# Two late experts' rows, the final norm's factors and a POOL drain in the tail of a mixture-of-experts layer

## The chip, the core and the metric

The kernel runs on one core of a Trainium2 chip. The metric is device time of one execution in microseconds (us). Work is spread over five engines: PE (matrix products), DVE and ACT (elementwise work), POOL (here mostly gathers and scatters) and SP (which only issues transfers). The 16 DMA engines of the core move data. Each engine works through its own list of instructions in order; semaphores make it wait for others.

## What is computed

One layer of a diffusion backbone over 512 latent tokens with 1024 features: a gated linear attention mixer, then a grouped top-2 mixture of 16 experts, then a final RMSNorm. Only the last two concern this change:

```python
for e in range(N_EXPERTS):
    he = jax.nn.silu(h @ w1[e]) * (h @ w3[e])
    out = out + gates[:, e:e + 1] * (he @ w2[e])
...
x = x + g2 * f.reshape(bsz, t, D_MODEL)
...
return _rmsnorm(x, final_g)
```

`_rmsnorm` divides each row by the root of its mean square and multiplies it by `final_g`. A token goes to two experts, so a row of `x` gets two sums, and its norm needs both.

## The kernel before, in words

Experts are sorted by how many tokens they got; the first run with many rows, the last two (the late ones, here **p** and **q**, list places 14 and 15) hold at most 32 rows each. For each expert POOL gathers its rows, PE multiplies them by gate and up weights ("up", halves a and b) and by the down weights ("down"), DVE scales the result by gate and `g2`, and POOL adds it by an indirect scatter to the accumulator `accd` in DRAM (L1106). SP streams the weights, 1 MB a load (L688). `load_unit` gives each load a dependency on the landing of the load three before it, so at most three are in flight. The scheduler also uses eight completion lanes (DMAHW0 to DMAHW7) in turn for transfers issued by SP and ACT: a transfer that takes a lane waits until the lane's last one has landed.

For p and q the scatter is left out. The tail, whose order on all engines is written out by hand, does this instead:

- `finish_consts` (on ACT and its queue) lays out `g2` and loads `final_g` to all 128 partitions with one transfer (L1330) into a buffer that the compiler calls `srg`.
- `late_consts` builds 0/1 matrices: `hot` (which accumulator row belongs to which late row) and `same` (which row of p is the same token as which row of q). A key is transposed on PE and compared on DVE.
- `finish_load` reads `accd` back in four tiles of 128 rows (L1341, B and su) once the scatter of expert 13, the last one that goes to `accd`, has landed. `squares` (ACT, L1344), `finish_scale` and `finish_out` (DVE, L1351; store on SP, L1352) norm these 512 rows and store them. The rows of p and q are stored there too, still without the late sums.
- `late_rows` picks the accumulator rows of p and q out of the four tiles by products with `hot`. `late_other` adds, by a product with `same`, the other late expert's sum where both have the token.
- `late_out` norms the rows of p and q and stores them over the earlier ones with two indirect stores from POOL (L1401). They write to `out`, so the first waits for the landing of the four tile stores, and the second for the landing of the first. The norm is over quarters of a row that lie in four partition groups, and a product with `SELP` sums their squares.

A `G.drain()` (L1435) stands in the tail's code. It depends on nothing, and in the built program of before it sits near the start of POOL's list. After the tail comes a loop that runs zero times for these inputs (L1513) and the end of the program (L1556), where POOL has a drain of its own.

Of the kernel before, what the change touches and what calls it, by code (L numbers as in the profile page):

```python
# [10 lines left out]
BF16 = mybir.dt.bfloat16  # L11
I32 = mybir.dt.int32
U8 = mybir.dt.uint8
AF = mybir.ActivationFunctionType
OP = mybir.AluOpType
# [3 lines left out]
P = 128  # L19
D = 1024  # L20
# [12 lines left out]
def dit_kernel(ctx: ExitStack, tc: tile.TileContext, I, out):  # L33
# [12 lines left out]
    def bank(p=None):  # L46
        p = p or pa
        return p.tile([P, 512], F32, tag="bk", name="bk")
# [1266 lines left out]
    def index_for(g):  # L1315
        c0 = cols[order[g[0]]][0][0]
        c1 = cols[order[g[-1]]][-1][0] + 1
        index_of(c0, tiles[c0:c1], lambda e: zp[:, :, e - NS], vals, wide=g[0] == 2)

    ss3, rstd3 = R("ss3", [4]), R("rstd3", [4])  # L1320
    fin = {}

    def finish_consts():
        f, e = free.pop(0), free.pop(0)
        fin["g"], fin["j"] = f[:, 0:1024], f[:, 1024:2048]
        fin["y"] = [u[:, h * 1024:h * 1024 + 1024] for u in (free.pop(0), free.pop(0)) for h in range(2)]
        fin["h"], fin["g2"], *fin["late"] = [e[:, k * 256:k * 256 + 256] for k in range(6)]
        fin["hot"] = [e[:, 1536 + 128 * k:1664 + 128 * k].rearrange("p (t s) -> p t s", t=4) for k in range(2)]
        fin["same"] = [e[:, 1792 + 128 * k:1920 + 128 * k] for k in range(2)]
        nc.scalar.dma_start(fin["g"], I["final_g"].rearrange("(o n) -> o n", o=1).partition_broadcast(P))  # L1330
        lay("g2", g2b)

    def lay(name, src):
        A = P // tiles[-1][2]
        for a in range(A):
            q, n = slice(P // A * a, P // A * (a + 1)), D // A
            S.copy(fin[name][q, 0:n], src[q, a * n:a * n + n])

    def finish_load(ts=range(4)):
        for t in ts:  # L1340
# [23 lines left out]
    for a in range(QA):  # L1364
        ia = ident[:, a * P // QA:(a + 1) * P // QA].unsqueeze(1).to_broadcast([P, QA, P // QA])
        V.tensor_add(sv, sv, ia) if a else V.tensor_copy(sv, ia)
    lrs, lsq, key = R("lrs", [2]), m1[:, 2:4], m1[:, 0:2]

    def late_consts(ts):
        c = NTL - 2  # L1370
        V.tensor_copy(key, gix2[:, c:c + 2])
        for k in range(2):
            for t in range(4):
                V.tensor_scalar(fin["hot"][k][:, t], iot[:, 0:32], zp[:, t, ND - 2 + k:ND - 1 + k], None, op0=OP.is_equal)
            pt = bank(pb)[:, 0:P]
            PE.transpose(pt, key[:, k:k + 1].to_broadcast([P, P]), ident)
            V.tensor_scalar(fin["same"][k], pt, key[:, 1 - k:2 - k], None, op0=OP.is_equal)

    def late_rows(ts, k):
        for i, t in enumerate(ts):  # L1380
# [1 line left out]
                t.rows, t.z = bank()[:, 0:t.n], fin["late"][2 + i]  # L1382
            t.groups(t.rows, fin["hot"][i][:, k], lambda a: fin["y"][k][:, a * t.n:a * t.n + t.n], k == 0, k == 3)

    def late_other(ts, i):
        pt = bank()[:, 0:ts[i].n]
        PE.matmul(pt, fin["same"][i], ts[1 - i].y, start=True, stop=True)
        return pt

    def late_out(ts):  # L1390
        for i, t in enumerate(ts):
            S.activation(mo.tile([P, 512], BF16, tag="ohx", name="jk3", bufs=NO)[:, 0:t.n], t.z, AF.Square, accum_out=lsq[:, i:i + 1])
        pt = bank(pb)
        PE.matmul(pt[:, 0:2], SELP, lsq, start=True, stop=True)
        rsqrt(lrs, pt[:, 0:2], 2, 1.0 / D, "x")
        for i, t in enumerate(ts):
            V.scalar_tensor_tensor(t.z, t.z, lrs[:, i:i + 1], fin["h"][:, 0:t.n], op0=OP.mult, op1=OP.mult)
            late_store(t)

    def late_store(t):  # L1400
        G.indirect_dma_start(out=parts(out[0], t.A), out_offset=bass.IndirectOffsetOnAxis(ap=t.idx, axis=0), in_=t.z, in_offset=None,  # L1401
# [2 lines left out]
    with tc.manual_schedule(engines={G.engine}):  # L1404
        ex = [Expert(cols[order[0]], True)]
        weights()
        ex.append(Expert(cols[order[1]]))
        ranked()
        for i in range(NE - 1):
            if i == 1:  # L1410
                ex[0].down(wts[0])
                with tc.issue_after(ex[0].tls[0].last.ins):
                    rest()
                    index_for(range(2, 4))
                ex[0].store()
            ex[i].up(wts[i], "a")
            while i and len(ex) < min(NE, i + 3):
                ex.append(Expert(cols[order[len(ex)]]))
            if i > 1:
                ex[i - 1].down(wts[i - 1])  # L1420
            ex[i].up(wts[i], "b")
            if i % 2 and i + 3 < NE:
                index_for(range(i + 3, min(i + 5, NE)))
            if i:
                ex[i - 1].scatter()

    finish_consts()
    tail = {G.engine, V.engine, S.engine, PE.engine, nc.sync.engine}
    with tc.manual_schedule(engines=tail):
# [2 lines left out]
        p.late, q.late = fin["late"][0:2]  # L1432
        q.by_exp = True
        pq = (p, q)
        G.drain()  # L1435
        late_consts(pq)
        p_.down(wts[NE - 2])
        S.preload_act_table_set("natural_log_exp_and_others")
        q_.up(wts[NE - 1], "a")
        load_unit(wts[NE - 1], regs[NE - 1], 4)  # L1440
        finish_load()
        for h in range(2):
            load_unit(wts[NE - 1], regs[NE - 1], 5, range(h, h + 1))
        S.copy(fin["late"][3], late_other(pq, 1))
        q_.up(wts[NE - 1], "b")
        q_.turn()
        for k in range(2):
# [6 lines left out]
            squares(k)  # L1454
            late_rows(pq, k)
        finish_scale(2)
        lay("h", fin["g"])
        V.tensor_add(p.z, p.y, p.rows)
        V.tensor_add(q.z, q.z, q.rows)
        finish_out(2)  # L1460
        q_.down(wts[NE - 1])
        V.tensor_add(q.z, q.z, q.y)
        V.tensor_add(p.z, p.z, late_other(pq, 0))
        finish_out(3)
        late_out(pq)


    ctx2 = ExitStack()
# [91 lines left out]
```

## Time and profile before

| | us |
|---|---|
| median of 3 runs (lowest to highest) | 661.37 (660.69 to 661.97) |
| the profiled execution | 660.54 |
| its span, first to last instruction | 658.7 |
| PE busy | 603.8 (92%) |
| DVE busy | 463.1 (70%) |
| ACT busy | 302.1 (46%) |
| POOL busy | 89.8 (14%) |

The profiled execution has 1.84 us around its span and is 0.83 us under the median. Rows of a timeline give start, duration, engine, line of the kernel, operation, what is written and read, count, and in brackets the idle time of the engine before and what ended it. A name with q behind it (SPq, POOLq) is the engine's sequencer.

### The profile page before, as it was taken

The numbers are of one execution on the slowest core, as the hardware profiler recorded it, in microseconds if no ns is written. First come the engines' busy times: TensorE is split into PE (matmuls) and PEld (weight loads), VectorE is DVE, ScalarE is ACT, GpSimd is POOL, SyncE is SP. The second block draws the span as 40 slices with busy tenths as digits, with TensorE's granted clock in tenths as the row PEclk, the third lists the DMA queues.
The fourth block names the chain that finished last, engine by engine and source line by source line (L and its number), as shares of the span: only waits on it lengthen the run. The fifth ranks groups of instructions, "written<-read, shape, count | busy, mean of one in ns | idle before, by whom it ended". The sixth has DMA issues, their size and how long they took to land. (4 is left out here: it accounts for less than half of the span.)

```text
span 658.7 us, 11293 instructions
## 1 busy us (share of the span) xinstructions
PE 603.8 (92%) x4266; PEld 415.1 (63%) x4266; DVE 463.1 (70%) x951; ACT 302.1 (46%) x512; POOL 89.8 (14%) x99
## 2 busy tenths in 40 slices
PE   3999999999999999999979989999999999999760
PEld 3777677776878878778757465446455657664320
DVE  5766599749976962664489398477799979994251
ACT  6334398266252334632441354345353657772150
POOL 3030000010100010013100232020321222331001
PEclk9999999999999999999979999999999999999985
DMA  8996572120235771577662989899999999999981
GB/s 275 341 350 208 194 253 65 66 65 3 90 106 194 256 254 49 208 256 291 256 237 63 402 306 360 336 343 344 369 378 400 368 345 365 401 387 365 325 336 44
DMA packets 50248, 168.87 MB, mean 256 GB/s; under 512 B 6738, under 2 KB 17100, under 8 KB 37136
## 3 DMA queue, kind: packets, MB, share of 16 engines
q1 hardware_dynamic: 43216, 156.26, 63.9%
q0 software_dynamic: 4880, 8.64, 5.5%
q10 hardware_dynamic: 2096, 3.23, 1.5%
q8 instruction: 34, 0.56, 0.3%
q14 instruction: 22, 0.18, 0.1%
HBM read 159.03 MB, written 12.30 MB: 260 GB/s over the span
## 5 line engine op out<-in xcount | busy, mean ns | idle before, releaser
L51 PE MATMUL bk<-wh,fh 128*128 128x512 f32 (+3 forms) x276 | 111.1, 409 | 0.7 <-ACT fh L56 0.4
L52 PE MATMUL bk<-wl,fh 128*128 128x512 f32 (+3 forms) x276 | 111.0, 404 | 0.0
L53 PE MATMUL bk<-wh,fl 128*128 128x512 f32 (+3 forms) x276 | 109.2, 400 | 0.5 <-DVE fl L57 0.5
L282 DVE TENSOR_TENSOR wl<-st,wh 128x512 fp32r<-128x512 f32 x60 | 39.8, 684 | 39.1 <-ACT wh L281 37.8
L56 ACT CAST wh<-su 128x1024 fp32r<-128x1024 f32 x45 | 46.7, 1047 | 39.7 <-PE bk L53 37.8
L281 ACT CAST wh<-st 128x512 fp32r<-128x512 f32 x60 | 35.9, 621 | 61.6 <-PE bk L53 51.1
L51 PEld LDWEIGHTS bk<-wh,fh 128*128 128x128 f32 (+3 forms) x276 | 50.1, 183 | 20.0 <-ACT wh L56 3.4
L52 PEld LDWEIGHTS bk<-wl,fh 128*128 128x128 f32 (+3 forms) x276 | 50.7, 184 | 16.0 <-DVE wl L57 2.5
L57 DVE TENSOR_TENSOR wl<-su,wh 128x1024 fp32r<-128x1024 f32 x45 | 54.5, 1221 | 8.1 <-ACT wh L56 6.7
L53 PEld LDWEIGHTS bk<-wh,fl 128*128 128x128 f32 (+3 forms) x276 | 50.5, 183 | 13.7 <-issue 1.2
L1106 POOL DMA_INDIRECT accd<-y,gix x15 | 34.3, 2290 | 157.9 <-DVE y L1166 86.8
L56 ACT CAST fx<-su 128x1024 fp32r<-128x1024 f32 x21 | 22.0, 1049 | 21.9 <-PE bk L53 21.7
L1202 PE MATMUL bk<-su,xg 128*32 128x256 f32 (+1 forms) x216 | 30.4, 457 | 1.5 <-DVE xg L1196 1.5
L57 DVE TENSOR_TENSOR fx<-su,fx 128x1024 fp32r<-128x1024 f32 x21 | 25.6, 1221 | 5.6 <-ACT fx L56 5.3
L51 PE MATMUL bk<-fx,fh 128*128 128x512 f32 (+3 forms) x68 | 27.9, 410 | 1.2 <-ACT fh L56 1.2
L52 PE MATMUL bk<-fx,fh 128*128 128x512 f32 (+3 forms) x68 | 27.4, 402 | 1.0 <-DVE fx L57 1.0
L53 PE MATMUL bk<-fx,fl 128*128 128x512 f32 (+3 forms) x68 | 26.6, 394 | 0.2 <-DVE fl L57 0.2
L1102 POOL DMA_INDIRECT xg<-h2d,gix x16 | 19.7, 1232 | 40.0 <-DVE pis L1005 15.4
L1202 PE MATMUL bk<-su,he 128*64 128x512 f32 (+1 forms) x136 | 21.6, 497 | 0.9 <-DVE he L1226 0.8
L250 POOL DMA_DIRECT2D mrd<-mrow x8 | 3.8, 487 | 129.4 <-DVE mrow L248 129.4
L52 PE MATMUL bk<-fl,wh 128*128 128x512 f32 x48 | 19.8, 412 | 0.0
L53 PE MATMUL bk<-fh,wl 128*128 128x512 f32 x48 | 19.7, 411 | 0.0
(486 smaller groups left out, 1284.9 us busy)
## 6 DMA issues: line engine op xcount, KB each, us to landing
su<-in_w_up_e_dram SPq DMA_DIRECT2D x23, 1024.0 KB, 8.3
su<-in_w_down_e_dram SPq DMA_DIRECT2D x21, 1024.0 KB, 7.9
su<-in_w_gate_e_dram SPq DMA_DIRECT2D x19, 1024.0 KB, 7.6
st<-in_gla_w_in_dram SPq DMA_DIRECT2D x10, 1024.0 KB, 5.4
QQ<-in_w_mod_dram SPq DMA_DIRECT2D x5, 1024.0 KB, 10.2
st<-in_w_gate_e_dram SPq DMA_DIRECT2D x5, 1024.0 KB, 8.1
st<-in_w_up_e_dram SPq DMA_DIRECT2D x5, 1024.0 KB, 9.4
B<-in_w_mod_dram SPq DMA_DIRECT2D x4, 1024.0 KB, 4.8
```

Source lines behind the costliest of these rows:

```text
L51: PE.matmul(o, ah, bh, start=first, stop=False)
L52: PE.matmul(o, ah, bl, start=False, stop=False)
L53: return PE.matmul(o, al, bh, start=False, stop=last)
L56: S.copy(hi, full)
L57: return V.tensor_sub(lo, full, hi.bitcast(F32))
L250: G.dma_start(mrd[4 * h_ + c4:4 * h_ + c4 + 1, :], mrow[32 * c4:32 * c4 + 1, :])
L281: S.copy(w[0][:, k], st[:, k])
L282: mark[0] = V.tensor_sub(w[1][:, k], st[:, k], w[0][:, k].bitcast(F32))
L1102: G.indirect_dma_start(out=xg, out_offset=None, in_=src, in_offset=bass.IndirectOffsetOnAxis(ap=idx, axis=0), bounds_check=n - 1, oob_is_e ...
L1106: G.indirect_dma_start(out=dst, out_offset=bass.IndirectOffsetOnAxis(ap=idx, axis=0), in_=y, in_offset=None, bounds_check=n - 1, oob_is_er ...
L1202: PE.matmul(o[s.w * a:s.w * a + s.w], l, r(a), start=first, stop=last, tile_position=(0, s.w * a))
```

## The change

Six edits, all in the tail:

1. `final_g` is loaded into one partition (4 KB in place of 512 KB), after `g2` is laid out. A new function, `finish_g`, spreads it to 128 partitions by two products with a row of ones and two copies from PSUM. It stands between p's down and q's up.
2. Only one `same` matrix is built (one transpose and one compare fewer). p's rows are stored with the accumulator's rows and p's own sum alone; q's rows get both sums. A token that both have is stored twice, the second time, by q's store, in full.
3. `late_out` is called for p and for q apart. p's call stands ahead of q's down.
4. The last `finish_out` stands straight behind the third, ahead of everything of q.
5. `lay("h", ...)`, which spreads `final_g` for the late rows, stands behind `finish_out`; on ACT it keeps its place.
6. `G.drain()` stands at the end of the block that orders POOL's list, behind expert 13's scatter.

```diff
+    one = raw2[0:1, :]
...
-        fin["g"], fin["j"] = f[:, 0:1024], f[:, 1024:2048]
+        fin["g"], fin["j"], fin["row"] = f[:, 0:1024], f[:, 1024:2048], f[0:1, 1024:2048]
...
-        nc.scalar.dma_start(fin["g"], I["final_g"].rearrange("(o n) -> o n", o=1).partition_broadcast(P))
+        nc.scalar.dma_start(fin["row"], I["final_g"].rearrange("(o n) -> o n", o=1))
+        V.memset(one, 1.0)
...
+    def finish_g():
+        for a in range(2):
+            sl = slice(a * 512, a * 512 + 512)
+            pt = bank()
+            PE.matmul(pt, one, fin["row"][:, sl], start=True, stop=True)
+            S.copy(fin["g"][:, sl], pt)
...
-            pt = bank(pb)[:, 0:P]
-            PE.transpose(pt, key[:, k:k + 1].to_broadcast([P, P]), ident)
-            V.tensor_scalar(fin["same"][k], pt, key[:, 1 - k:2 - k], None, op0=OP.is_equal)
+        pt = bank(pb)[:, 0:P]
+        PE.transpose(pt, key[:, 1:2].to_broadcast([P, P]), ident)
+        V.tensor_scalar(fin["same"][0], pt, key[:, 0:1], None, op0=OP.is_equal)
...
+    def late_out(t, i):
+        ss, n = m1[:, 2 + i:3 + i], t.n
+        S.activation(mo.tile([P, 512], BF16, tag="ohx", name="jk3", bufs=NO)[:, 0:n], t.z, AF.Square, accum_out=ss)
         pt = bank(pb)
+        PE.matmul(pt[:, 0:1], SELP, ss, start=True, stop=True)
+        rsqrt(lrs[i], pt[:, 0:1], 1, 1.0 / D, "x")
+        V.scalar_tensor_tensor(t.z, t.z, lrs[i], fin["h"][:, 0:n], op0=OP.mult, op1=OP.mult)
+        late_store(t)
...
+        G.drain()
...
-        G.drain()
         late_consts(pq)
         p_.down(wts[NE - 2])
         S.preload_act_table_set("natural_log_exp_and_others")
+        finish_g()
         q_.up(wts[NE - 1], "a")
...
-        lay("h", fin["g"])
         V.tensor_add(p.z, p.y, p.rows)
         V.tensor_add(q.z, q.z, q.rows)
         finish_out(2)
+        finish_out(3)
+        lay("h", fin["g"])
+        late_out(p, 0)
         q_.down(wts[NE - 1])
         V.tensor_add(q.z, q.z, q.y)
-        V.tensor_add(p.z, p.z, late_other(pq, 0))
-        finish_out(3)
-        late_out(pq)
+        late_out(q, 1)
```

The first place is SP's list, at the weights of q: `su_2693` is the up weights of q's half a, the two `st` are half b, `su_2696` is half of its down weights. Names in brackets are the semaphores waited for, and the transfer of `final_g` sits on lane DMAHW1 before and on DMAHW2 now. One piece of the difference:

```order
 L688 DMA su_2700<-in_w_gate_e_dram 128x2048 [waits DMAHW5_49,PE_49]
 L688 ISA
-L688 DMA su_2693<-in_w_up_e_dram 128x2048 [waits DMAHW6_49,DMAHW1_49,PE_49]
-L688 ISA
-L688 DMA st<-in_w_gate_e_dram 128x2048 [waits DMAHW7_49,DVE_49]
+L688 DMA su_2693<-in_w_up_e_dram 128x2048 [waits DMAHW6_49,PE_49]
+L688 ISA
+L688 DMA st<-in_w_gate_e_dram 128x2048 [waits DMAHW7_49,DMAHW2_49,DVE_49]
```

The wait for `final_g` has moved from the load of half a's up weights to the next load.

The second place is DVE's list at the end of the tail: L1351 (L1360 in the change) is `finish_out`, L1234 q's sum, L1462 and L1463 the additions to the late rows, L136 to L129 the roots, L1397 (L1400) the scaling of the late rows. Before:

```order
L1351 SCALAR_TENSOR_TENSOR su_2692<-su_2692,rstd_3377,srg 128x1024
L1234 SCALAR_TENSOR_TENSOR srg<-bk,gsl,srg 128x256
L1462 TENSOR_TENSOR srg<-srg 128x256
L1463 TENSOR_TENSOR srg<-srg,bk 128x256
L1351 SCALAR_TENSOR_TENSOR su_2692<-su_2692,rstd_3377,srg 128x1024
L136 TENSOR_SCALAR rsv<-bk 128x2
L127 TENSOR_TENSOR rst<-lrs 128x2
L128 SCALAR_TENSOR_TENSOR rst<-rst,rsv 128x2
L129 SCALAR_TENSOR_TENSOR lrs<-rst,lrs 128x2
L1397 SCALAR_TENSOR_TENSOR srg<-srg,lrs 128x256 x2
```

and in the change:

```order
L1360 SCALAR_TENSOR_TENSOR su_2692<-su_2692,rstd_3377,srg 128x1024 x2
L136 TENSOR_SCALAR rsv<-bk 128x1
L127 TENSOR_TENSOR rst<-lrs_3382 128x1
L128 SCALAR_TENSOR_TENSOR rst<-rst,rsv 128x1
L129 SCALAR_TENSOR_TENSOR lrs_3382<-rst,lrs_3382 128x1
L1400 SCALAR_TENSOR_TENSOR srg<-srg,lrs_3382 128x256
L1234 SCALAR_TENSOR_TENSOR srg<-bk,gsl,srg 128x256
L1470 TENSOR_TENSOR srg<-srg 128x256
L136 TENSOR_SCALAR rsv<-bk 128x1
L127 TENSOR_TENSOR rst<-lrs_3383 128x1
L128 SCALAR_TENSOR_TENSOR rst<-rst,rsv 128x1
L129 SCALAR_TENSOR_TENSOR lrs_3383<-rst,lrs_3383 128x1
```

The fourth tile's scaling has moved up to the third's, p's roots and scaling come next, and q's sum, roots and scaling (a last row L1400) are behind them.

The third place is PE's list from the accumulator's rows on (L1202 with B_86 and su_2692 are `late_rows`, L1202 with su_2696 and su_2697 is q's down, L1398 the product with `SELP`, L1449 that with `same`). One piece of the difference:

```order
-L1387 MATMUL bk<-srg 128x256
+L1449 MATMUL bk<-srg 128x256
 L1202 MATMUL bk<-st,xg 32x256 x16
 L1215 MATMUL bk<-ident,he 128x128 x2
 L1202 MATMUL bk<-B_86,srg 32x256 x16
 L1202 MATMUL bk<-su_2692,srg 32x256 x16
+L1398 MATMUL bk<-m_3230,wr 128x1
 L1202 MATMUL bk<-su_2696,he 32x256 x8
 L1202 MATMUL bk<-su_2697,he 32x256 x8
-L1387 MATMUL bk<-srg 128x256
-L1394 MATMUL bk<-m_3230,wr 128x2
```

p's product with `SELP` now stands ahead of q's down, and q's own one behind it takes the place of the second `same` product and of the common one.

## Rows read from the trace of the kernel before

**Rows 1.** The chain of work that ended last, in the stretch from 600 us to the end: start, duration, what.

```profile
646.24 1.05 DMA out_dram<-srg,gix
...
649.73 0.72 POOL out_dram L1401
```

**Rows 2.** Instructions of the lines 1401 and 1556 on POOL: count, duration in ns (min/median/max), first and last start in us.

```profile
L1401 POOL DMA_INDIRECT out_dram<-srg,gix x2: 1023/1035/1047, 646.2 to 649.4; - x2
...
L1556 POOLq DRAIN  x3: 52/105/4723, 653.2 to 658.5; - x3
```

**Rows 3.** The other drain of POOL (line 1435), the POOL instructions ahead of it from its timeline, the landing of the four transfers of line 234 (from issue, us), and the packets that POOL's transfers (q0) made up to 12.6 us and from then to the end.

```profile
L1435 POOLq DRAIN  x1: 7363/7363/7363, 5.2 to 5.2; - x1
...
5.37 2.02 POOL L234 DMA_DIRECT2D mrow<-in_b_mod_dram  x4
...
7.49 0.20 POOL L431 IOTA ix<- 128x32 int32 x1
...
DMA to landing us min/median/max: 5.2/5.7/5.9
...
q0 software_dynamic: 288, 0.15, 6.0%
...
q0 software_dynamic: 4592, 8.49, 5.5%
```

**Rows 4.** Timelines of DVE and POOL at the end.

```profile
638.48 1.28 DVE L1351 SCALAR_TENSOR_TENSOR su<-su,rstd,srg 128x1024 f32<-128x1024 f32 x1
639.67 0.48 DVE L1234 SCALAR_TENSOR_TENSOR srg<-bk,gsl,srg 128x256 f32<-128x256 f32 x1
...
641.28 1.28 DVE L1351 SCALAR_TENSOR_TENSOR su<-su,rstd,srg 128x1024 f32<-128x1024 f32 x1
...
644.17 0.88 DVE L1397 SCALAR_TENSOR_TENSOR srg<-srg,lrs 128x256 f32<-128x256 f32 x2
...
616.57 1.57 POOL L1106 DMA_INDIRECT accd<-y,gix  x1 [11.59 <-DVE y L1240]
646.24 1.05 POOL L1401 DMA_INDIRECT out_dram<-srg,gix  x1 [28.10 <-SPq L1513]
649.43 1.02 POOL L1401 DMA_INDIRECT out_dram<-srg,gix  x1 [2.14 <-issue]
```

**Rows 5.** DMA issues of the stores, each from a window that holds that one: KB, us from issue to landing. In order: the second tile store (issued at 637.39), the third (639.78), p's store, q's store.

```profile
out_dram<-B SPq DMA_DIRECT2D x1, 512.0 KB, 3.2
...
out_dram<-su SPq DMA_DIRECT2D x1, 512.0 KB, 2.6
...
out_dram<-srg,gix POOLq DMA_INDIRECT x1, 2.4
...
out_dram<-srg,gix POOLq DMA_INDIRECT x1, 2.8
```

**Rows 6.** SP around the weights of q: the load of half a's up weights in its timeline, its wait from 608.0 us on (line 688, duration in ns), what its queue waited for (us), and the landing of `final_g` (issued at 604.35).

```profile
614.64 0.33 SPq L688 DMA_DIRECT2D su<-in_w_up_e_dram  x1
...
L688 SPq EVENT_SEMAPHORE  x1: 6560/6560/6560, 608.0 to 608.0; - x1
...
SPq L688 <- DMA srg<-in_final_g_dram: 8.5, 1, 8.5
...
srg<-in_final_g_dram ACTq DMA_DIRECT2D x1, 512.0 KB, 10.2
```

**Rows 7.** Busy time in stretches: us; PE, PEld, DVE, ACT, POOL busy (instructions); granted clock, busy share of the DMA engines, GB/s.

```profile
613.50:616.50 3.00, 3.00 (x38) 1.08 (x34) 1.50 (x2) 0.00 (x0) 0.00 (x0) 1.00 0.44 113
...
622.50:624.00 1.50, 1.50 (x18) 0.57 (x10) 0.00 (x0) 0.22 (x1) 0.00 (x0) 1.00 1.04 340
...
632.30:635.65 3.35, 3.21 (x32) 1.59 (x36) 1.42 (x5) 3.07 (x8) 0.00 (x0) 0.50 0.96 336
```

**Rows 8.** The scatter of expert 13 (issued at 616.57), the last load of q ahead of the accumulator's (619.65) and the first accumulator tile (626.25): KB, us to landing.

```profile
accd<-y,gix POOLq DMA_INDIRECT x1, 9.6
...
su<-in_w_down_e_dram SPq DMA_DIRECT2D x1, 1024.0 KB, 8.8
...
B<-accd SPq DMA_DIRECT2D x1, 512.0 KB, 4.9
```

**Rows 9.** Timelines of PE and ACT from p's down to the squares.

```profile
620.17 0.44 PE L1194 MATMUL bk<-ident,xg 128*128 128x128 f32 x2
...
626.01 1.92 PE L1202 MATMUL bk<-st,xg 128*32 128x256 f32 x28 [1.72 <-DMA st<-in_w_up_e_dram]
...
628.94 0.28 ACT L1220 ACTIVATE he<-bk 128x128 f32<-128x128 f32 x1 [0.59 <-PE bk L1215]
631.15 1.06 ACT L1344 ACTIVATE srg<-B 128x1024 f32<-128x1024 f32 x1 [1.93 <-DMA B<-accd]
...
611.08 3.65 PE L1202 MATMUL bk<-su,he 128*64 128x512 f32 x16
```

**Rows 10.** ACT and PE at the norm of the late rows.

```profile
636.89 1.63 ACT L1337 COPY srg<-srg 32x256 f32<-32x256 f32 x4
641.40 0.42 ACT L1392 ACTIVATE jk<-srg 128x256 bf16<-128x256 f32 x1 [2.88 <-DVE srg L1463]
...
636.65 2.07 PE L1202 MATMUL bk<-su,he 128*32 128x256 f32 x32
...
642.36 0.47 PE L1394 MATMUL bk<-m,wr 128*128 128x2 f32 x2 [1.46 <-ACT jk L1392]
```

More of the change, by code (lines that the diff above doesn't have):

```diff
@@ L1366, in dit_kernel @@
         V.tensor_add(sv, sv, ia) if a else V.tensor_copy(sv, ia)
-    lrs, lsq, key = R("lrs", [2]), m1[:, 2:4], m1[:, 0:2]
+    lrs, key = [R("lrs%d" % k, [1]) for k in range(2)], m1[:, 0:2]
     def late_consts(ts):
@@ L1383, in late_rows @@
             t.groups(t.rows, fin["hot"][i][:, k], lambda a: fin["y"][k][:, a * t.n:a * t.n + t.n], k == 0, k == 3)
[L1385 to L1392, printed above, removed]
-        pt = bank(pb)
[L1394 to L1398, printed above, removed]
+    def late_out(t, i):
+        ss, n = m1[:, 2 + i:3 + i], t.n
+        S.activation(mo.tile([P, 512], BF16, tag="ohx", name="jk3", bufs=NO)[:, 0:n], t.z, AF.Square, accum_out=ss)
+        pt = bank(pb)
+        PE.matmul(pt[:, 0:1], SELP, ss, start=True, stop=True)
+        rsqrt(lrs[i], pt[:, 0:1], 1, 1.0 / D, "x")
+        V.scalar_tensor_tensor(t.z, t.z, lrs[i], fin["h"][:, 0:n], op0=OP.mult, op1=OP.mult)
+        late_store(t)
     def late_store(t):
@@ L1443, in dit_kernel @@
             load_unit(wts[NE - 1], regs[NE - 1], 5, range(h, h + 1))
-        S.copy(fin["late"][3], late_other(pq, 1))
+        both_ = bank()[:, 0:q.n]
+        PE.matmul(both_, fin["same"][0], p.y, start=True, stop=True)
+        S.copy(fin["late"][3], both_)
         q_.up(wts[NE - 1], "b")
```

## The prediction

> **What bounds the kernel now.** I read the chain that ended last first, from the end backwards. It holds the two indirect stores from POOL and nothing after them [rows 1]. So the edits matter as far as they bring q's store forward, or shorten what follows it. From q's store (649.43) to the end of the span (658.7) it is 9.3 us, of which one instruction, a drain of POOL at 653.2, takes 4.72 [rows 2, 4].
>
> Next I read what holds the two stores. DVE is done with both late rows at 644.17 + 0.88 = 645.05, but POOL starts p's store at 646.24, 1.2 us later, while the scatter of expert 13 started 0.3 us after its data [rows 4]. So p's store waits for something else: the landing of the fourth tile store. That one can go out when DVE has scaled the tile, at 641.28 + 1.28 = 642.56; tile stores land after 2.6 to 3.2 us [rows 4, 5], at 645.2 to 645.8. q's store starts 3.2 us after p's, of which 2.4 are p's landing and 0.8 POOL's start behind a landing [rows 4, 5]. The chain at the end is therefore: fourth tile scaled, landed, p's store, landed, q's store, landed, end.
>
> What holds the tile work is the accumulator. ACT waits until 631.15 for its first tile [rows 9], which SP could ask for only when the scatter of expert 13 had landed, 9.6 us after 616.57 [rows 8]. Before that, SP stood from 608.0 to 614.6 at one load of q's weights and waited for the landing of `final_g`, 10.2 us after its issue [rows 6]. The DMA engines ran dry behind it: between 613.5 and 616.5 they were busy for 44% and moved 113 GB/s, where the full stretch at 622.5 shows 340 GB/s [rows 7].
>
> **The change part by part.**
>
> *The load of `final_g`.* 512 KB become 4 KB. At 340 GB/s this saves 0.52 MB / 340 GB/s = 1.5 us of DMA time. The wait for the lane moves to the next load, but the load of half a's up weights can go at 608.0. It fills the dry stretch, which lost 3.0 x (1 - 113/340) = 2.0 us. So the stream of q's weights is up to 3.5 us further by 616.5. The row has no like in the trace; if it landed after as long as the 512 KB did, 10.2 us, the next load would go at about 615, still ahead of the end of the megabyte in front of it.
>
> How much of the 3.5 us reaches the squares? At 616.57, when the scatter is issued, some 1.7 us less of weights stands in front of it (three loads are in flight at most, and the oldest is nearly done in place of just begun). Say the scatter lands 1.7 us sooner, at 624.5. The last weight load ahead of the accumulator's, landed at 619.65 + 8.8 = 628.45 before [rows 8], would land near 626.4, earlier by 2.0. Then the first tile needs 512 KB more and lands at 628.3 to 629.0, not 631.15. Lower bound: the scatter lands as before, SP asks at 626.25, finds the queue empty, and the 3.2 us of a tile store with another in front [rows 5] give 629.5 to 629.7, a gain of 1.4. Upper bound: ACT cannot start the squares ahead of q's exponential, which ended at 629.22 [rows 9] and follows PE. PE gets new work, below, but no longer waits 1.72 us for half b's up weights [rows 9]; with the 0.9 us of new work that brings the exponential forward by 0.8, so the gain is at most 631.15 - 628.4 = 2.7. I take **2.2 us**, nearer the upper end, because all of the idle stretch lies ahead of the scatter.
>
> The Trainium skill, "DMA: Bandwidth & Descriptors", section "Queues, rings and completion order", says that a DMA engine takes turns between the queue rows that have work, a packet at a time. By that, the scatter on POOL's row would share with the weights as long as there are any, however many stand there, and would land near 626.2 again; the sum would be 2.7 in place of 3.5. The 9.6 and 10.2 us of transfers under a full queue [rows 6, 8] fit either reading.
>
> *Spreading by a product.* Two products of 128 x 512 and two copies. Eight products of 512 columns took 3.65 us [rows 9], so two cost 0.9 on PE, ahead of q's transposes at 620.17. The cover is the 1.72 us wait behind them; were the weights as late as before, the 0.9 would cost nothing either. ACT is idle there for its copies. The bounds are 0 and 0.9; the limit of 2.7 above has it in full.
>
> *One `same` matrix less, p without q's sum.* A transpose, a compare, a 256-column product and an addition less. The first three lie beside other work. The addition (0.42) stood between the third and the fourth tile and is part of the next step.
>
> *The fourth tile straight behind the third.* Its scaling started at 641.28; the place behind the third is 639.67, where q's sum stood [rows 4]. So it is scaled 1.6 us sooner. Its store then goes out 1.2 us behind the third's instead of 2.8, like the second behind the first, which took 3.2 us to land where the third took 2.6 [rows 5]. Landing is sooner by 1.2 to 1.6; I take **1.3 us**. p's store waits for this landing and q's for p's, so both move with it.
>
> *p and q apart.* Is q ready in time? In times of the trace of before, without the first term: the copies of `h` end at 638.5 [rows 10], p's squares (0.42 and a read) at 639.1, p's product with `SELP` at 639.6 [rows 10]; only then PE begins q's down (2.07), to 641.6. DVE does the fourth tile to 640.95, p's roots and scaling to 642.75, q's sum and addition (0.48, 0.42) to 643.65. From squares to scaling before took 644.17 - 641.40 = 2.8 us [rows 4, 10], and one scaling 0.44, so q is ready at 646.9. p's store now starts at 645.0 and q's at 648.1, each 1.3 sooner. So q has 1.2 us to spare; and if PE ran q's down at the lower level of its clock (granted 0.50, 32 products in 3.21 us [rows 7], not 2.07), 1.1 more would still be covered. The step costs nothing. If the cover went, every us would count in full.
>
> *The drain.* It now stands behind expert 13's scatter, so POOL starts it near 616.57 + 1.57 = 618.1. Nobody needs POOL until p's store at about 642. Queued behind it are the two stores alone. Does it shorten the drain at the end? That one takes 4.72 us [rows 2] though all stores had landed (649.43 + 2.8 = 652.3 [rows 4, 5]) when it began. The early one ran on until 5.16 + 7.36 = 12.5. POOL's last instruction ahead of it ended at 7.69 [rows 3]: 4.8 us. So both fit a fixed piece of work of 4.7 to 4.8 us, whatever was transferred before: 288 packets there, 4592 here [rows 3]. Drains with nothing between take 52 and 105 ns [rows 2]. Two stores lie between the moved one and the last, so by this reading the last again takes 4.7. I take **0**; the other end is 4.72 - 0.1 = 4.6.
>
> Sum: 2.2 + 1.3 + 0 = 3.5 us from the profiled execution's 660.54, hence 657.0. That execution is 0.8 under the median of the runs, so the median to expect is 661.4 - 3.5 = **657.9 us**.
>
> **The rivals.**
>
> *The drain does pay.* The early drain also fits another reading: it waits for the last landing (the last of the four transfers was issued at about 6.9 and landed 5.2 later, at 12.1 [rows 3]) and then needs 0.4 us. By that, the 4.72 at the end is work piled up since: 16 times the packets, 11 times the time. The moved drain would do it behind the scatter, unseen, and about 0.4 would be left at the end: 4.3 less, 653.6. For it: work that grows with what was transferred needs no coincidence of 4.7 and 4.8. Against it: it needs two effects where one number explains both drains.
>
> *The scatter lands as late as before*, at 626.2, because it is held by the queue being busy and not by how much stands in it. Then the first term is 1.4, the gain 2.7, the time 658.7. For it: 9.6 us for the scatter and 10.2 for 512 KB [rows 6, 8], nearly alike with the queue full in both cases. Against it: less stands in front now. This is what the rule of the Trainium skill's page above comes to.
>
> *The front gives nothing.* The accumulator's tiles land as before, because PE's 0.9 us and the moved lane wait eat the stream's gain. Then only 1.3 is left: 660.1. Against it: the dry stretch is real, and q's weights are wanted by nobody before 621.
>
> *The drain blocks POOL.* On POOL nothing can pass it. If it waits for more than POOL's own transfers, p's store is late. This decides from 642 - 618 = 24 us of drain on; beyond that every us counts. At 31 us the kernel would be 7 - 3.5 = 3.5 us slower, 664.9. The longest drain shown is 7.4 [rows 3], and its wait for the scatter would end near 626.
>
> **How the numbers follow.** Forecast 0.40, a drain that pays 0.33, a scatter as late as before 0.13, no gain in front 0.08, a blocking drain 0.04, other 0.02. The forecast's own range, with the scatter's case, is 1.4 + 1.2 to 2.7 + 1.6 of gain, 657.1 to 658.8. The range over the cases runs from the paying drain with the upper ends, 661.4 - 4.3 - 4.6 = 652.5, to 659.5, where the forecast's lower end and a run's spread of 0.7 end; it leaves out most of the last three cases. A measurement of this kernel can tell about 0.2%, 1.3 us. Faster by more: 0.40 + 0.33 + 0.13 and half of the case with no gain in front, 0.90. Within: 0.05. Slower: 0.05.
>
> **What the profile after would show.** SP's load of half a's up weights at about 608, no dry stretch near 615, the first squares between 628.4 and 629.8; the fourth tile's scaling right behind the third's; p's store 3.5 us sooner than 646.24, q's 3.2 behind it; a drain of line 1429 from 618 on. The drain at the end decides between 657.9 and 653.6. I am wrong if q's store starts well after p's has landed (then q's own chain is last), if ACT's squares do not move, or if POOL's drain ends after 640.

## The result and the profile after

After: 655.42 us median of 4 runs (653.35 to 656.01). Before, on the same chip: 661.03 (660.69 to 661.97). The ratio is 0.9907, 95% interval 0.9883 to 0.9932: faster by 6.1 us (4.5 to 7.7). Forecast were 657.9, and 653.6 by the rival in which the drain pays; the measured time lies between the two. The profiled execution is the fastest of the four (653.35, span 651.2), and one experiment below shows what it was spared.

The end first. Timeline of POOL after, the counterpart of [rows 4], with the scatter of expert 12 ahead of it:

```profile
603.51 1.46 POOL L1106 DMA_INDIRECT accd<-y,gix  x1 [10.22 <-DVE y L1166]
615.92 1.57 POOL L1106 DMA_INDIRECT accd<-y,gix  x1 [10.95 <-DVE y L1240]
643.02 1.05 POOL L1404 DMA_INDIRECT out_dram<-srg,gix  x1 [25.53 <-DVE srg L1470]
646.23 1.02 POOL L1404 DMA_INDIRECT out_dram<-srg,gix  x1 [2.16 <-DVEq L1519]
```

The drains of POOL after, against [rows 2]: the final ones (line 1562) and the moved one (line 1429), each with count, ns (min/median/max), first and last start:

```profile
L1562 POOLq DRAIN  x3: 52/105/218, 650.0 to 650.9; - x3
...
L1429 POOLq DRAIN  x1: 11867/11867/11867, 615.7 to 615.7; - x1
```

The long one of the final three went from 4723 to 218 ns. The moved one lasts 11.9 us, to 627.5, 2.7 us past the scatter's landing (624.9), and nobody wants POOL before 643. From q's store to the end of the span there are 5.0 us where there were 9.3.

The two stores come 3.2 us sooner than in [rows 4], where 3.5 were forecast. Of that, 0.65 is a gain that the forecast doesn't have: the scatter itself went out at 615.92, not 616.57, though expert 12's scatter ahead of it stands where it stood. Before:

```profile
603.52 1.46 POOL L1106 DMA_INDIRECT accd<-y,gix  x1 [10.22 <-DVE y L1166]
```

From the one scatter to the other it is 13.05 us in the kernel before and 13.05 to 13.06 in e2 and e4 below, which load `final_g` as it does; it is 12.40 to 12.42 in after and in all ten other runs, which have the new front (the one-row load and the spreading). So the front brings expert 13's scatter forward by 0.64 us; by which of its edits, no run separates. Where expert 12's scatter stands differs by up to 2.5 us between executions, so places are counted below from the issue of expert 13's scatter, and this 0.64 is not in them. p's store is at 27.10 behind it, before at 29.67: 2.6 us sooner.

Where the front's part stopped. Stretches, columns as in [rows 7]:

```profile
613.50:616.50 3.00, 2.48 (x37) 0.98 (x33) 1.50 (x2) 0.37 (x1) 0.58 (x1) 1.00 0.97 374
622.50:624.00 1.50, 1.50 (x20) 0.82 (x21) 0.00 (x0) 0.00 (x0) 0.00 (x0) 0.59 0.72 189
624.00:625.50 1.50, 1.50 (x16) 0.44 (x8) 0.00 (x0) 0.00 (x0) 0.00 (x0) 0.50 0.09 16
625.50:627.00 1.50, 1.50 (x18) 0.82 (x18) 0.00 (x0) 0.37 (x1) 0.00 (x0) 0.77 0.59 210
```

The dry stretch at 613.5 is full now (374 GB/s, before 113), and a new one stands at 622.5 to 627. Behind it is SP's wait for the scatter, from SP's waits (us in total, times, longest):

```profile
SPq L1350 <- DMA accd<-y,gix: 8.2, 1, 8.2
...
SPq L688 <- DMA srg<-in_final_g_dram: 4.5, 1, 4.5
```

The second row is the lane's wait (8.5 in [rows 6]), which the one-row load still costs (its landing let SP go on at 611.6, as foreseen "still ahead of the end of the megabyte in front of it"). The scatter's issue and landing, against [rows 8]:

```profile
accd<-y,gix POOLq DMA_INDIRECT x1, 9.0
```

It was 9.6. The last weights ahead of the accumulator landed 3.7 us sooner (624.7, before 628.5), while the scatter's time shrank by 0.6. Next, PE and then ACT on the way to the squares, against [rows 9]:

```profile
619.51 1.98 PE L1345 MATMUL bk<-srg,raw 1*128 1x512 f32 x4
...
622.38 3.31 PE L1202 MATMUL bk<-su,xg 128*32 128x256 f32 x32 [0.52 <-DVE xg L1196]
...
626.51 1.93 PE L1202 MATMUL bk<-st,xg 128*32 128x256 f32 x32
...
638.10 3.64 PE L1202 MATMUL bk<-su,he 128*32 128x256 f32 x32
```

```profile
629.47 0.28 ACT L1220 ACTIVATE he<-bk 128x128 f32<-128x128 f32 x1 [0.59 <-PE bk L1215]
629.77 1.06 ACT L1353 ACTIVATE srg<-B 128x1024 f32<-128x1024 f32 x1
```

The two spreading products (a product in f32 shows as two records, x4 in all) take 1.98 us, not 0.9. Half a of q's up, 32 records, takes 3.31 instead of 1.93: the granted clock is 0.50 to 0.59 in the stretches from 622.5 to 625.5, the lower level of 1.2 GHz. Ahead of that PE had run the spreading products and q's two transposes and stood idle for 0.52 us. So q's exponential is later than before (13.55 us behind the scatter's issue, before 12.37), and the squares follow it with no idle time; before they waited 1.93 us for the accumulator. DVE on the two last tiles and on q, against [rows 4]:

```profile
636.95 2.48 DVE L1360 SCALAR_TENSOR_TENSOR su<-su,rstd,srg 128x1024 f32<-128x1024 f32 x2
...
641.80 0.48 DVE L1234 SCALAR_TENSOR_TENSOR srg<-bk,gsl,srg 128x256 f32<-128x256 f32 x1 [0.68 <-PE bk L1202]
...
645.28 0.48 DVE L1400 SCALAR_TENSOR_TENSOR srg<-srg,lrs 128x256 f32<-128x256 f32 x1
```

The fourth tile stands right behind the third. q is ready at 645.76, p has landed at 645.4 (2.4 us behind its issue), and q's store starts 0.8 behind that landing, as before. With the 0.3 us from data to store that [rows 4] show, q could have gone at 646.06: of the 1.2 us to spare 0.2 were there, because q's down (638.10) ran at half clock.

### The profile page after: what moved, and what is told of

Its sections match the earlier page's. It is cut to its first block, busy times and chain, and to the rows that moved or that the text cites. A ratio compares the mean times of both kernels' runs of the same rounds, so it can differ in the third digit from the quotient of the medians.

```text
span 651.2 us, 11308 instructions
## 1 busy us (share of the span) xinstructions
PE 606.6 (93%) x4269; PEld 416.4 (64%) x4269; DVE 462.9 (71%) x954; ACT 303.8 (47%) x516; POOL 90.3 (14%) x99
## 5 line engine op out<-in xcount | busy, mean ns | idle before, releaser
L53 PEld LDWEIGHTS bk<-wh,fl 128*128 128x128 f32 (+3 forms) x276 | 50.5, 183 | 13.6 <-issue 1.2
L1202 PE MATMUL bk<-su,xg 128*32 128x256 f32 (+1 forms) x216 | 31.8, 487 | 1.5 <-DVE xg L1196 1.5
L1202 PE MATMUL bk<-su,he 128*64 128x512 f32 (+1 forms) x136 | 23.1, 556 | 1.6 <-DVE he L1226 1.6
L1202 PEld LDWEIGHTS bk<-su,xg 128*32 128x32 f32 (+1 forms) x216 | 9.9, 124 | 15.9 <-issue 12.9
L1240 DVE SCALAR_TENSOR_TENSOR y<-bk,gsl,g1b 64x512 f32<-64x512 f32 (+1 forms) x14 | 9.4, 672 | 14.6 <-PE bk L1202 14.5
```

What stands on the lines that cost most here:

```text
L53: return PE.matmul(o, al, bh, start=False, stop=last)
L1202: PE.matmul(o[s.w * a:s.w * a + s.w], l, r(a), start=first, stop=last, tile_position=(0, s.w * a))
L1240: s.mark = V.scalar_tensor_tensor(y[q], s.py[q], s.gs[q], g2b[q, a * s.n:a * s.n + s.n], op0=OP.mult, op1=OP.mult)
```

## The experiments

All times are medians; "before" is the median of the kernel before on the same chip as the run beside it. The chips differ from group to group, so runs of different groups are compared by their ratios. "Squares", "p" and "q" come from one execution, the profiled one: first squares and p's store in us behind the issue of expert 13's scatter, q's store behind p's.

| kernel | us | before | ratio (95%) | squares | p | q |
|---|---|---|---|---|---|---|
| before | 661.0 | | | 14.6 | 29.7 | 3.2 |
| after | 655.42 | 661.03 | 0.9907 (0.9883 to 0.9932) | 13.9 | 27.1 | 3.2 |
| e1_drain_back | 660.33 | 661.81 | 0.9968 (0.9945 to 0.9990) | 12.8 | 28.0 | 3.2 |
| e2_drain_only | 657.62 | 661.81 | 0.9931 (0.9905 to 0.9958) | 15.9 | 31.1 | 3.2 |
| e3_front_only | 660.96 | 661.81 | 0.9981 (0.9964 to 0.9999) | 13.7 | 29.3 | 3.2 |
| e4_stores_only | 661.41 | 661.81 | 0.9986 (0.9964 to 1.0008) | 13.8 | 27.7 | 5.0 |
| e5_drain_mid | 656.64 | 661.60 | one execution | 13.6 | 27.3 | 4.9 |
| e6_hold | 656.99 | 661.60 | 0.9930 (0.9904 to 0.9957) | 13.5 | 30.7 | 3.2 |
| e7_g_late | 655.62 | 661.60 | 0.9916 (0.9889 to 0.9942) | 12.5 | 26.5 | 4.6 |
| e8_both | 655.81 | 661.60 | 0.9924 (0.9901 to 0.9947) | 11.9 | 28.8 | 3.3 |
| e9_after_again | 656.05 | 661.24 | 0.9913 (0.9882 to 0.9943) | 14.7 | 28.1 | 4.9 |
| e10_fill | 657.22 | 661.24 | 0.9947 (0.9928 to 0.9967) | 15.8 | 29.5 | 4.8 |
| e12_touch | 655.33 | 661.24 | 0.9912 (0.9880 to 0.9944) | 13.9 | 27.5 | 3.2 |
| e13_late_touch | 653.53 | 662.46 | 0.9862 (0.9843 to 0.9881) | 12.8 | 26.5 | 3.2 |

### The drain: e1, e2, e5

e1, on the changed kernel:

```diff
                 ex[i - 1].scatter()
-        G.drain()
...
         pq = (p, q)
+        G.drain()
         late_consts(pq)
```

> The changed kernel with the drain of POOL put back where it stood before (at the head of the tail, where it runs near the start of the program). Theory A, work that piles up with what POOL transferred since the last drain: the drain at the end takes 4.7 us again in place of 0.22, and the time is the changed kernel's 655.4 + 4.3 to 4.5 = 659.8. Rival B, the drain at the end got short because the two late stores and the tile stores stand otherwise now: it stays at 0.2 us and the time at 655.4. Rival C, the short drain of the changed kernel is paid in its other executions elsewhere (they are 2 to 2.6 us above the profiled one): 657.5 to 658.

e2 is the same edit the other way round, on the kernel before.

> The kernel before with one edit: the drain of POOL behind expert 13's scatter. Theory A (work piled up): the drain at the end 0.2 us in place of 4.72, time 661.0 - 4.3 = 656.7; q's store starts where it did. Rival B (the new order of the stores made it short): 4.7 us at the end again and 661.0.

The final drains of e1, then the moved and the final ones of e2:

```profile
L1562 POOLq DRAIN  x3: 52/105/4723, 653.0 to 658.3; - x3
```

```profile
L1426 POOLq DRAIN  x1: 12528/12528/12528, 615.9 to 615.9; - x1
...
L1556 POOLq DRAIN  x3: 52/105/218, 654.4 to 655.3; - x3
```

4723 ns wherever the drain stands at the head, 218 wherever it stands behind expert 13, with either order of the stores. Theory A holds, B falls: e2, the drain alone, is 4.6 us faster by the ratio (2.8 to 6.3), e1, all the rest without it, 2.1 (0.7 to 3.6). Rival C falls too: e1 is at 660.3, not at 657.5 to 658.

e5 asks what the work is.

```diff
+            if i == 7:
+                G.drain()
-        G.drain()
```

> The changed kernel with its drain behind the scatter of expert 6 instead of expert 13, half of POOL's late transfers earlier. Theory A1, the end pays for every transfer since the last drain, alike for each: the drain at the end lies halfway between 0.22 and 4.72 us, 2.0 to 3.0. Theory A2, the end pays only for what is beyond some number, or for the first transfers of the program: 0.2 to 1. Theory A3, it is one fixed price wherever a transfer under a full queue came after the last drain: 4.7. The time itself may be longer for another reason (the gathers of the next experts stand behind the drain), so only the drain is read.

Its drains, and POOL's transfers from 509 us to the end:

```profile
L1430 POOLq DRAIN  x1: 12067/12067/12067, 499.3 to 499.3; - x1
...
L1563 POOLq DRAIN  x3: 52/105/1279, 652.4 to 654.2; - x3
```

```profile
accd<-y,gix POOLq DMA_INDIRECT x7, 11.1
xg<-h2d,gix POOLq DMA_INDIRECT x6, 10.2
out_dram<-srg,gix POOLq DMA_INDIRECT x2, 3.5
```

Those are 15 transfers since the last drain, for 1279 ns. After has 2, for 218; the kernel before has 57 (33 indirect ones, 24 small ones), for 4723. (1279 - 218) / 13 = 82 ns; (4723 - 1279) / 42 = 82 ns. By packets it is no line: 96, 1584 and 4592 packets give 0.71 ns for each of the first step and 1.15 of the second. With none, 52 lies on the same line (52 + 2 x 82 = 216). So A1's form holds, 82 ns for each transfer that POOL issued since its last drain. My figure of 2.0 to 3.0 was wrong, since I had not counted: 15 of 57 lie behind expert 6, not half.

### Front and stores apart: e3, e4

e3, on the kernel before: `final_g` as a row, and

```diff
+        finish_g()
         q_.up(wts[NE - 1], "a")
```

> The kernel before with the front alone: final_g loaded as one row of 4 KB and spread by two products. As the prediction put it: 2.2 us sooner, 661.0 - 2.2 = 658.8 (bounds 1.4 to 2.7). As the trace of the changed kernel reads (the squares wait for q's exponential, which PE brings only 0.7 us sooner): 660.3. If the spreading products cost as much as the stream gains: 661.0.

e4, on the changed kernel: the drain as in e1, and `final_g` as before.

```diff
-        nc.scalar.dma_start(fin["row"], I["final_g"].rearrange("(o n) -> o n", o=1))
-        V.memset(one, 1.0)
+        nc.scalar.dma_start(fin["g"], I["final_g"].rearrange("(o n) -> o n", o=1).partition_broadcast(P))
...
-        finish_g()
```

> The kernel before with the order of the stores alone: one matrix, p stored without q's sum, the fourth tile straight behind the third; final_g in 512 KB and the drain where they were. As the prediction put it: 1.3 us sooner, 659.7 (1.2 to 1.6). As the changed kernel's trace reads (fourth tile 3.1 us sooner in all, less 0.65 of an earlier scatter and 0.7 of the front): 1.8 us, 659.2. The drain at the end stays at 4.7 by theory A and is short by rival B (then 655.0).

e3 gives 1.3 us by the ratio (0.1 to 2.4), 0.85 by the medians, with the 0.64 of the earlier scatter in it; its squares start right behind q's exponential, as in after. That is what the changed kernel's trace said, and less than the 2.2 predicted, though the interval just holds 2.2. e4 gives 0.9 by the ratio (-0.5 to 2.4), 0.4 by the medians, so its interval holds zero: p's store is 2.0 us sooner, but q's comes 5.0 behind p's in place of 3.2. The timeline of POOL, and p's store with its landing:

```profile
643.89 1.05 POOL L1403 DMA_INDIRECT out_dram<-srg,gix  x1 [26.09 <-SPq L1517]
648.84 1.02 POOL L1403 DMA_INDIRECT out_dram<-srg,gix  x1 [3.90 <-issue]
```

```profile
out_dram<-srg,gix POOLq DMA_INDIRECT x1, 4.2
```

p landed after 4.2 us, not 2.4. q was scaled at 645.66 and waited 3.2 us for that. Its drain at the end is 4723 ns long.

### What holds the squares: e6, e7, e8, e10

e6 and e7, on the changed kernel; e8 has both edits.

```diff
-        load_unit(wts[NE - 1], regs[NE - 1], 4)
         finish_load()
+        load_unit(wts[NE - 1], regs[NE - 1], 4)
```

> The changed kernel with one load held back: the first megabyte of q's down weights is asked for behind the accumulator's four tiles. Theory S, the scatter lands 9.0 us after its issue because weight packets are asked for all the time it runs: with a megabyte less it lands near 622 and not 624.9, the accumulator's first tile at 625, but the squares still wait for q's exponential at 629.5, so 0 to 0.5 us sooner, 655.0. Rival, the scatter's time is its own (its packets start 4.7 us behind the issue and last 4 us whatever stands beside them): it lands at 624.9 again, the down weights come 2 us later, 656 to 657.

```diff
-        finish_g()
         q_.up(wts[NE - 1], "a")
...
         q_.turn()
+        finish_g()
...
-            S.copy(fin["g"][:, sl], pt)
+            V.tensor_copy(fin["g"][:, sl], pt)
```

> The changed kernel with the two spreading products behind q's activation, the copies on DVE, so that q's up products stand 1.98 us sooner. Theory P, the squares wait for q's exponential and that for PE's chain with the two products in it: the exponential ends at 627 to 628 in place of 629.75, the squares start at the accumulator's first tile, 628.2 to 629, and the kernel is 0.8 to 1.5 us sooner, 654.2. Rival, q's exponential waits for the weights' landing and not for PE: no change, 655.4; or the products now stand in front of the late rows' products on PE and the kernel is up to 2 us later, 657.4.

> The changed kernel with both: the down weights held back and the spreading products behind q's activation. If the squares have two holders, the scatter (theory S) and PE's chain (theory P), only both together move them: accumulator's first tile at 625, exponential at 627 to 628, squares from 627.5, 2 us sooner: 653.4, unless q's down weights (the last loads) become the last wait ahead of q's store, which gives 654.5 to 655.4. If the scatter's time is its own, the same as with the products alone or 1 us more.

ACT in e7:

```profile
627.17 0.28 ACT L1220 ACTIVATE he<-bk 128x128 f32<-128x128 f32 x1 [0.59 <-PE bk L1215]
629.63 1.06 ACT L1353 ACTIVATE srg<-B 128x1024 f32<-128x1024 f32 x1 [2.18 <-DMA B<-accd]
```

q's exponential starts 10.05 us behind the scatter in place of 13.55, and the squares wait for the accumulator again, 1.3 us sooner than in after. So in after PE's chain held the squares, as theory P has it. That takes the half clock too: in e1, with the products in the same place and half a at full clock (1.93 us), the exponential starts 11.9 behind the scatter, and the squares (12.8) wait 0.57 us for the accumulator. e7 is not faster than after, though; in its profiled execution p's landing takes 3.8 us.

In e8 the scatter lands 6.8 us behind its issue, with no weights asked for while it runs. In e6 it takes 9.6, where the last load in front happened to go out 1.0 behind it, so e6 doesn't test theory S; in time it came out as its rival said (656.99), with p's store 3.6 us later than in after. So theory S holds in e8, against the rival that the scatter's time is its own, but moves no time (the ten runs of e8 lie between 653.9 and 660.5): the held megabyte now runs beside the tile stores, and the second needs 7.4 us to land (3.2 in [rows 5]). The scatter of e8 and its second tile store:

```profile
accd<-y,gix POOLq DMA_INDIRECT x1, 6.8
...
out_dram<-B SPq DMA_DIRECT2D x1, 512.0 KB, 7.4
```

e10 goes the other way: e7, the last megabyte ahead of the accumulator's tiles, and q's down ahead of p's norm.

```diff
         load_unit(wts[NE - 1], regs[NE - 1], 4)
+        load_unit(wts[NE - 1], regs[NE - 1], 5)
         finish_load()
-        for h in range(2):
-            load_unit(wts[NE - 1], regs[NE - 1], 5, range(h, h + 1))
...
+        q_.down(wts[NE - 1])
         late_out(p, 0)
-        q_.down(wts[NE - 1])
```

> The changed kernel with three moves: the spreading products behind q's activation with copies on DVE, the last megabyte of q's down weights asked for ahead of the accumulator's tiles (into the dry stretch at 622.5 to 627), and q's down products ahead of p's product with SELP. Theory: the dry stretch costs the end of the stream, so the tile stores and q's down weights come sooner and PE does q's down right behind the late rows at its full clock; squares from 12.5 us behind the scatter's issue (13.9 in the changed kernel), fourth tile at 22.9, p's store at 25.8 (27.1), q's at 29.0, the instruction packet behind p's packets: 652.5 to 654. Rival: with a megabyte more in the queue the scatter lands later than 9.0 us (9.6 or more) and the accumulator shares the queue with it: squares as late as in the changed kernel, 655 to 656.5.

The rival held in its mechanism: the scatter lands after 9.7 us, and the squares wait for the accumulator until 15.8 behind its issue, later than the rival said. With three moves in one run, what each did stays open. The scatter, and ACT's first squares:

```profile
accd<-y,gix POOLq DMA_INDIRECT x1, 9.7
```

```profile
631.52 1.06 ACT L1353 ACTIVATE srg<-B 128x1024 f32<-128x1024 f32 x1 [3.61 <-DMA B<-accd]
```

### What p's landing hangs on: e9, e12, e13

e9 is the changed kernel, unedited.

> The changed kernel once more, unedited. Theory F: a 16 KB packet of instructions (queue q8) goes out 2.05 to 2.08 us behind the start of q's product with SELP; where it falls on p's packets, 1.6 to 2.1 us behind the issue of p's store, p lands after 3.8 to 4.2 us in place of 2.4, and q's store waits for that. In the profile read before it missed them by 0.3 us. By F another execution shows p landing after 3.8 to 4.2 and some 655.3 us in all, or after 2.4 and some 653.5, with the packet at 1.2 to 2.0 us behind p's issue in the first case and outside in the second. Rival: the 2 us between the profiled execution and the other three lie ahead of the scatter (start of the program); p lands after 2.4 us in any case.

e9's p store, and what the DMA queues started in the 0.2 us from 647.4 on (packets, MB, share of 16 engines):

```profile
out_dram<-srg,gix POOLq DMA_INDIRECT x1, 4.1
...
q8 instruction: 1, 0.02, 34.6%
q0 software_dynamic: 16, 0.02, 34.1%
```

One packet of 16 KB of instructions, on one DMA engine for 0.346 x 16 x 0.2 = 1.1 us, stands between p's packets (p was issued at 645.55). In after the same packet started at 645.42, 2.40 behind p's issue, when p's packets (1.61 to 2.08) were through. In eleven profiles it can be set beside p's landing: at 1.62, 1.64, 1.66, 1.95 and 2.02 us behind p's issue (e7, e4, e5, e9, e10) p took 3.8, 4.2, 4.2, 4.1 and 4.0 us; at 2.11 and 2.40 (e1, after), at 3.92 and 4.07 (e12, e13), and ahead of p's issue (-1.03 in e6, -0.18 in e8) it took 2.4 to 2.5. In each of the five hit, the last of p's packets starts some 0.2 us behind the end of the instruction packet. q's store waits for that landing, so a hit costs 1.4 to 1.8 us. In the kernel before the packet starts 1.2 us ahead of p's store and is through by then. The Trainium skill, "DMA: Bandwidth & Descriptors", section "Queues, rings and completion order", has a DMA engine finish a packet of one queue row before it turns to the next; p's wait behind one long packet agrees.

e12 tests who asks for the packet: the changed kernel and, as PE's last instruction,

```diff
         late_out(q, 1)
+        PE.matmul(bank(pb)[:, 0:1], SELP, q.z[:, 0:1], start=True, stop=True)
```

> The changed kernel with one small product more, on q's scaled rows, whose result nobody reads, so that PE's last instruction comes some 2.5 us later. Theory F with PE as the engine that asks for the instruction packet: the packet goes out some 2.1 us behind this product, p lands after 2.4 us, and the packet falls on q's store, which lands after up to 4.2 us in place of 2.85: 655 to 656. If another engine asks for it, it stays about 2.05 us behind q's product with SELP, and p's landing is 2.4 or 3.8 to 4.2 as in the changed kernel.

PE's last products in e12, POOL's stores, and the queues' packets in the 0.2 us from 647.5 on with q's store (issued 646.90):

```profile
643.25 0.44 PE L1398 MATMUL bk<-m,wr 128*128 128x1 f32 x2 [2.74 <-ACT jk L1396]
645.57 0.59 PE L1472 MATMUL bk<-srg,wr 128*128 128x1 f32 x2 [1.88 <-DVE srg L1400]
```

```profile
643.69 1.05 POOL L1404 DMA_INDIRECT out_dram<-srg,gix  x1 [25.98 <-SPq L1520]
646.90 1.02 POOL L1404 DMA_INDIRECT out_dram<-srg,gix  x1 [2.16 <-DVEq L1520]
```

```profile
q8 instruction: 1, 0.02, 43.8%
...
out_dram<-srg,gix POOLq DMA_INDIRECT x1, 3.5
```

The packet went out 2.05 us behind the new last product and 4.4 behind the old one: it follows PE's end. p is spared (q's store 3.2 behind it), q pays 0.7 (3.5 in place of 2.8). On time alone e12 and e9, on the same chip, can't be told apart.

e13 takes e7 and puts PE's last product earlier, on q's norm factors:

```diff
         late_out(q, 1)
+        PE.matmul(bank(pb)[:, 0:1], SELP, lrs[1], start=True, stop=True)
```

> The changed kernel with the spreading products behind q's activation (copies on DVE) and one small product more on PE, on q's norm factors once they are done, whose result nobody reads. Theory: p's store starts 26.5 us behind the scatter's issue (27.1 to 28.1 in the changed kernel); the instruction packet goes out some 1.9 us behind that product, 3.2 to 3.5 us behind p's issue, after p's packets and, at 1.0 to 1.4 us long, mostly before q's (4.8 to 5.7); p lands after 2.4 us, q after 2.8 to 3.1: the profiled end is 1.4 us sooner than that of the products moved alone, and the median 654 to 654.5. Rival: the median stays at 655.3 to 656, because the executions differ by more ahead of the tail, or because PE's products in front of the late rows run at half clock and give it back.

POOL in e13, and the landings of p's and of q's store:

```profile
642.69 1.05 POOL L1404 DMA_INDIRECT out_dram<-srg,gix  x1 [24.97 <-DVE srg L1470]
645.90 1.02 POOL L1404 DMA_INDIRECT out_dram<-srg,gix  x1 [2.16 <-DVEq L1520]
```

```profile
out_dram<-srg,gix POOLq DMA_INDIRECT x1, 2.4
...
out_dram<-srg,gix POOLq DMA_INDIRECT x1, 3.3
```

e13 beats both kernels: 653.53 us (653.23 to 654.11), 8.9 us under the kernel before on its chip by the medians, and its ratio lies below those of after and of e7 with no overlap of the intervals, if barely (0.9881 against 0.9883 and 0.9889; three chips). The packet, 4.07 behind p's issue, still brushes q's. In its tail it is what the profiled execution of after was by luck.

## Why the prediction was right or wrong

*The drain, "I take 0".* Wrong, and the largest error: 4.6 us (e2). The reading of "a fixed piece of work of 4.7 to 4.8 us" rested on two drains of like length. The early one was a wait for a landing (it lasted 7.4 to 7.8 us in before, e1, e3 and e4 and ended 0.9 to 1.0 us behind the end of POOL's last packet each time); the last one was 57 transfers at 82 ns. "The drain does pay" described both, with the price 4.3 (the final drain itself fell by 4.5), and said of itself that work growing with the transfers "needs no coincidence". I gave it 0.33 and the coincidence 0.40; it should have been the other way.

*The load of `final_g`, "I take 2.2 us".* The mechanism was right as far as the queue: the load at 606.5, the dry stretch filled. The size was off: 1.3 us by e3 (0.1 to 2.4). The squares came 1.4 us sooner in the profiled execution, the lower bound, but 0.65 of that is the scatter's earlier issue, which no term of the sum has. Two steps failed. "The scatter lands 1.7 us sooner": it landed 0.6 sooner after and 0.8 in e3. The rival "the scatter lands as late as before" was nearer; e8 shows that the time depends on loads asked for while it runs (6.8 us with none, 8.8 to 9.6 with one megabyte, 9.5 with two in e9, 9.7 with three in e10; from one load on, runs of one kind differ as much as the counts do). That the queue rows take turns, as the Trainium skill's "DMA: Bandwidth & Descriptors", section "Queues, rings and completion order", has it, agrees with that. And the upper bound, "with the 0.9 us of new work that brings the exponential forward by 0.8", became the wrong way round: the exponential came 1.2 us later against the scatter's issue, and so set the squares.

*Spreading by a product, "the bounds are 0 and 0.9".* The products took 1.98 us, over the upper bound, because their like was wrongly chosen. The eight products of [rows 9], which are expert 13's down, have 64 output columns each (`128*64`) and overlap: 16 records with a mean of 598 ns fit into 3.65 us. A record of the spreading lasts as long (613 ns), but takes all 128 columns (`1*128`), and the four come one after another. The like was a product on all 128 columns; the trace of before has one, of 256 columns:

```profile
623.04 0.70 PE L1387 MATMUL bk<-srg 128*128 128x256 f32 x2
```

In after the products held the squares together with the half clock behind them, 1.3 us against e7; at full clock (e1) they held nothing. What the half clock owes to them is open. It stands behind them in after (3.31 us for half a), e3 (3.37), e5 (3.36) and e12 (3.35), in part in e9 (2.69), not in e1 and e6 (1.93), and in e2 there is some without them.

*The fourth tile straight behind the third, 1.3 us.* Right for p's store: it came 2.0 us sooner in e4's profiled execution, of which the squares give 0.7, so 1.3 are the step's.

*p and q apart, "the step costs nothing".* Wrong in the executions that the packet hits. The slack of q's own chain held in time, if barely (0.2 of 1.2 us). But the new order puts the end of PE's program, and with it an instruction packet, 1.6 to 2.4 us behind p's store, on p's packets or just past them (with the down weights held back, in e6 and e8, ahead of them). It is a cost of 1.4 to 1.8 us in the executions that are hit (e4, e5, e7, e9, e10). How much of the way from the 3.5 forecast to the 2.1 of front and stores together (e1; its interval reaches 3.6) is owed to such hits is not shown: e1's own profiled execution was missed by the packet, by 0.03 us.

*The sum.* 657.9 and 655.4 differ by a gain that I left out (4.6) and gains that I put too high (3.5 against some 2.1). The two errors have opposite signs, and that they cancel in part is luck. The measured time lies outside the forecast's own range (657.1 to 658.8); it lies in the range over the cases, 652.5 to 659.5, because that range took in the drain that pays. So the number is no support for the forecast's mechanism. *The drain blocks POOL* was wrong as expected: it ended 2.7 us past the scatter's landing.

Open: the four times of after span 2.7 us, those of e9, the same kernel, 3.7, and only two executions of this kernel have a trace. One was hit and one was not; how often, and how much of the span lies ahead of the tail (the scatter's issue moves between 615.7 and 618.0 over all profiles), was not separated. Nor is it shown why the moved drain ends 2.7 us behind the scatter's landing.

## What to carry to other kernels

Count the transfers that POOL has issued since its last drain: each costs 82 ns at the end of the program, and a drain put where POOL is idle for long enough (it lasted 9.7 to 12.6 us here, behind a scatter on its way) takes that price out of sight. For a product's price, take a like that uses as many output columns: products on fewer can overlap. Two like durations are no evidence of a fixed cost until a third case with another count has been found. Where small transfers wait for each other at the end, look also at what the engines themselves fetch there: moving PE's last instruction by some 2.5 us (e13 against e7) moved a 16 KB packet off p's store.

## What was not expected of the hardware

- A drain of POOL: 52 to 105 ns with nothing since the last one, 218 with 2 transfers, 1279 with 15, 4723 with 57.
- A packet of 16 KB of instructions starts 2.0 to 2.8 us behind the start of PE's last product, holds one DMA engine for 0.9 to 1.5 us, and makes an indirect store of 48 packets land after 3.8 to 4.2 us and not 2.4 when it falls among them.
- Two products of 512 columns in f32 with 128 output columns take 1.98 us, where eight with 64 output columns, which overlap, took 3.65 [rows 9].
- In all eleven runs with the new front, the scatter of expert 13 stands 0.64 us nearer to that of expert 12 than in the kernel before and in e2 and e4.
- A row of 4 KB, asked for behind full queues, landed after 5.5 us (after).
